# Grouped-query scores as rounded products over all rows, with separate column passes for keys and queries

## Chip, cores and metric

The kernel runs on one core of a Trainium2 chip. The metric is device time in microseconds (us) of one launch. TensorE is written PE, VectorE DVE, ScalarE ACT, GpSimd POOL, and SyncE, which issues DMAs, SP.

## What is computed

The reference is a two-layer diffusion backbone over 512 latent tokens and a context of 256 tokens, D_MODEL = 1024. Each layer mixes tokens by four branches; the one that matters here is grouped-query attention (GQA) with 4 query heads, 2 key heads and a head size of 64:

```python
kc_g, vc_g = rms_norm(split_heads(dc_k, D_KV_HEADS), k_norm), split_heads(dc_v, D_KV_HEADS)
q_g = rope_2d(rms_norm(split_heads(d_q, D_HEADS), q_norm), ang_r, ang_c)
k_g = rope_2d(rms_norm(split_heads(d_k, D_KV_HEADS), k_norm), ang_r, ang_c)
y_d = gqa_latent(q_g, k_g, split_heads(d_v, D_KV_HEADS), kc_g, vc_g)
...
s = jnp.einsum('bqkgd,bskd->bkgqs', qi, k_all).astype(jnp.float32) * d ** -0.5
p = jax.nn.softmax(s, axis=-1).astype(v_all.dtype)
return jnp.einsum('bkgqs,bskd->bqkgd', p, v_all)
```

Latent queries read all 768 keys; in layer 0 context queries read the 256 context keys (no rotary turn for context). The outputs are float32, and so are the scores of the reference.

## The kernel before

Tokens come in TI = 6 tiles of 128: tiles 0 and 1 are context, 2 to 5 latent. `qtiles` is 0 to 5 in layer 0 and 2 to 5 in layer 1, where context has no output. Nearly all matrix products are float32 written as three rounded products (`mm3`, L240 to L247): each operand is split into a rounded high part and a rounded remainder of type float32r, and high by high, high by low and low by high are summed in PSUM. `wload` (L209 to L220) makes the two parts of a weight: ACT casts (L219), DVE subtracts (L220, the weight remainder `wl`).

A static order of instructions per engine is made at build time by the tile framework from its own estimates of durations; each engine then runs its list in order and waits on semaphores. PSUM tiles come from small pools: `pm` 2, `pl` 2, `pq` 3, `po` 1.

`gqa(fill, fill2)` (L1170 to L1254) works in four steps:

1. Keys and values: per tile a projection `tm(W, 0, 256, h, i)` of 24 rounded products of 128x256, whose two halves ACT copies to `k2` and DVE to `v` (both parts of the tile `dkv`).
2. Queries: per tile the same projection, which ACT copies to `q4`.
3. The column pass, per tile: query and key heads together are squared (ACT), summed (DVE), brought through `rsqrt` (L450 to L462: a guess and three Newton rounds of three instructions), scaled by the norm weights, turned by the rotary angles (latent tiles: six DVE operations), transposed on PE (two transposes for queries, two for keys, whose heads ACT has copied twice, L1230) and copied to `qS` (ACT, L1236) and `kS` (DVE, L1237). Here dimensions lie on rows: two heads on two halves of 64 rows. Then `fill()` puts one gate unit into PE's work.
4. Attention, per key head `u` and pair of query tiles (`attend`, L976 to L1033): scores (`qk`, L1242 to L1244), maxima (L987 for context keys, L995 for latent keys), exponentials on ACT (L998, L1001), scaling by the sums, transposes of the probabilities (L1018), copies (L1023), products with the values (L1030). `fill2()` puts one gate unit behind each.

The score products are plain float32 over 64 rows: `mm(out_, qS[rows, u, ...], kS[rows, u, c0:c1])` with `rows` the half of head `hh`. The trace shows each as two passes.

`gate_unit` (L1258) computes sigmoid gates for 128 channels, independent of the attention: 24 products of 128x512 (latent) in both layers, and 24 of 128x256 (context) more in layer 0. There are 32 in a layer; `FILL[4]` and `FILL[5]` are 1.

Of the kernel before, what the change touches and what calls it, by code (L numbers as in the profile page):

```python
# [12 lines left out]
F32R = mybir.dt.float32r  # L13
U8 = mybir.dt.uint8
I32 = mybir.dt.int32
AF = mybir.ActivationFunctionType
ALU = mybir.AluOpType
AX = mybir.AxisListType
# [3 lines left out]
P = 128  # L22
# [5 lines left out]
TI = NT // P  # L28
# [8 lines left out]
EPS = 1e-6  # L37
# [52 lines left out]
def block_kernel(ctx, tc, t, out, dbg=None):  # L90
    nc = tc.nc
# [3 lines left out]
    def mark(label):  # L95
        cur[0] = label
        dbg.get("mark", lambda label: None)(label)
# [14 lines left out]
    def pm():  # L112
        return ps.tile([P, 512], F32, tag="pm", name=nm("pm"), bufs=2)
# [16 lines left out]
    mm = nc.tensor.matmul  # L130
# [217 lines left out]
    def tm(W, col, n, h, i):  # L348

        po = pl()[:, :n]  # L350
        mm3(po, h.sl(i * P, (i + 1) * P), [(a[:, col:col + n], b[:, col:col + n]) for a, b in W])
        return po
# [98 lines left out]
    def rsqrt(z, v, q):  # L451

        V = nc.vector
        V.tensor_scalar(z.bitcast(I32), v.bitcast(I32), -0.5, RS_GUESS, op0=ALU.mult, op1=ALU.add)
        one = z.shape[-1] == 1
        for c in RS:
            if one:
                V.scalar_tensor_tensor(q, z, v, z, op0=ALU.mult, op1=ALU.mult)
            else:
                V.tensor_tensor(q, z, z, op=ALU.mult)  # L460
                V.tensor_tensor(q, q, v, op=ALU.mult)
            V.scalar_tensor_tensor(z, q, -3.0 * c * c, z, op0=ALU.add, op1=ALU.mult)  # L462
# [52 lines left out]
    def mixing(l, h, hpool, W0):  # L515
# [9 lines left out]
        with tc.tile_pool(name=f"mx{l}", bufs=1, reuse_waits="tile") as mp:  # L525
            GB = 1552

            def g6(name, dt=F32):
                return mp.tile([P, GB], dt, tag="g", name=nm(name), bufs=12)


            def s2(shape):

                n = int(np.prod(shape[1:]))
                tl = mp.tile([P, 512], F32, tag="s", name=nm("s"), bufs=11)[:, :n]
                if len(shape) == 2:
                    return tl
                names = ["a", "b", "c", "d"][:len(shape) - 1]
                return tl.rearrange(f"p ({' '.join(names)}) -> p {' '.join(names)}", **dict(zip(names, shape[1:])))

            def small(shape, name, dt=F32, bufs=2):
                return mp.tile(shape, dt, tag=name, name=nm(name), bufs=bufs)
# [627 lines left out]
            def gqa(fill, fill2):  # L1170
                mark("gqa_cols")
                nw = small([P, 2, 64], "dnw", bufs=1)
                nc.scalar.dma_start(nw[:, 0, :], bcast_dram(t["q_norm"][l:l + 1, :], 64))
                nc.scalar.dma_start(nw[:, 1, :], bcast_dram(t["k_norm"][l:l + 1, :], 64))

                qS = g6("dq")[:, :1536].rearrange("p (h s) -> p h s", h=2)
                kS = g6("dk")[:, :1536].rearrange("p (h s) -> p h s", h=2)
                kv = g6("dkv")
                k2 = kv[:, :768].rearrange("p (i h e) -> p i h e", i=TI, h=2)
                v = kv[:, 768:1536].rearrange("p (i c) -> p i c", i=TI)  # L1180
                V = nc.vector
                q4 = g6("dq4")[:, :1536].rearrange("p (i h e) -> p i h e", i=TI, h=4)
                W = wchunk(w_in, [(O_DK, 256)])
                for i in range(TI):
                    po = tm(W, 0, 256, h, i)
                    nc.scalar.copy(k2[:, i], po[:, :128].rearrange("p (h e) -> p h e", h=2))
                    V.tensor_copy(v[:, i, :], po[:, 128:256])
                W = wchunk(w_in, [(O_DQ, 256)])
                for i in qtiles:
                    po = tm(W, 0, 256, h, i)  # L1190
                    nc.scalar.copy(q4[:, i], po.rearrange("p (h e) -> p h e", h=4))
                for i in range(TI):
                    h0 = 0 if i in qtiles else 4
                    x = s2([P, 6, 64])
                    sq = s2([P, 6, 64])
                    if h0 == 0:
                        nc.scalar.activation(sq[:, 0:4], q4[:, i], AF.Square)
                    nc.scalar.activation(sq[:, 4:6], k2[:, i], AF.Square)
                    ms = small([P, 6], "dms", bufs=2)
                    V.tensor_reduce(ms[:, h0:], sq[:, h0:], axis=AX.X, op=ALU.add)  # L1200
                    V.tensor_scalar(ms[:, h0:], ms[:, h0:], 1.0 / 64, EPS, op0=ALU.mult, op1=ALU.add)
                    r = small([P, 6], "drr", bufs=2)
                    c_ = small([P, 6], "drc", bufs=2)
                    rsqrt(r[:, h0:], ms[:, h0:], c_[:, h0:])
                    if h0 == 0:
                        V.tensor_tensor(x[:, 0:4], q4[:, i], r[:, 0:4].unsqueeze(2).to_broadcast([P, 4, 64]), op=ALU.mult)
                    V.tensor_tensor(x[:, 4:6], k2[:, i], r[:, 4:6].unsqueeze(2).to_broadcast([P, 2, 64]), op=ALU.mult)
                    if h0 == 0:
                        V.scalar_tensor_tensor(x[:, 0:4], x[:, 0:4], 0.125, nw[:, 0:1, :].to_broadcast([P, 4, 64]), op0=ALU.mult, op1=ALU.mult)
                    V.tensor_tensor(x[:, 4:6], x[:, 4:6], nw[:, 1:2, :].to_broadcast([P, 2, 64]), op=ALU.mult)  # L1210
                    if i >= 2:
                        yf = s2([P, 384])
                        y = yf.rearrange("p (h r w e) -> p h r w e", h=6, r=2, w=2)
                        x5 = x.rearrange("p h (r w e) -> p h r w e", r=2, w=2)
                        cs = rope[:, i - 2, 0].unsqueeze(1).to_broadcast([P, 6, 2, 16])
                        sn = rope[:, i - 2, 1].unsqueeze(1).to_broadcast([P, 6, 2, 16])
                        t1, t2 = (sq.rearrange("p h (a e) -> p (h a e)", a=2)[:, n * 192:n * 192 + 192].rearrange("p (h r e) -> p h r e", h=6, r=2) for n in range(2))
                        V.tensor_tensor(y[:, :, :, 0], x5[:, :, :, 0], cs, op=ALU.mult)
                        V.tensor_tensor(t1, x5[:, :, :, 1], sn, op=ALU.mult)
                        V.tensor_tensor(y[:, :, :, 0], y[:, :, :, 0], t1, op=ALU.subtract)  # L1220
                        V.tensor_tensor(y[:, :, :, 1], x5[:, :, :, 1], cs, op=ALU.mult)
                        V.tensor_tensor(t2, x5[:, :, :, 0], sn, op=ALU.mult)
                        V.tensor_tensor(y[:, :, :, 1], y[:, :, :, 1], t2, op=ALU.add)
                        yv = yf.rearrange("p (h e) -> p h e", h=6)
                    else:
                        yv = x
                    ts = slice(i * P, (i + 1) * P)
                    po = pm()
                    zk = s2([P, 2, 2, 64])
                    nc.scalar.copy(zk, yv[:, 4:6].unsqueeze(2).to_broadcast([P, 2, 2, 64]))  # L1230
                    for kvh in range(2):
                        if h0 == 0:
                            nc.tensor.transpose(po[:, kvh * P:(kvh + 1) * P], yv[:, 2 * kvh:2 * kvh + 2].rearrange("p h e -> p (h e)"), ident)
                        nc.tensor.transpose(po[:, 256 + kvh * P:384 + kvh * P], zk[:, kvh].rearrange("p w e -> p (w e)"), ident)
                    if h0 == 0:
                        nc.scalar.copy(qS[:, :, ts], po[:, :256].rearrange("p (h s) -> p h s", h=2))  # L1236
                    V.tensor_copy(kS[:, :, ts], po[:, 256:].rearrange("p (h s) -> p h s", h=2))  # L1237
                    fill()
                    mark("gqa_cols")
                new_out(3)  # L1240
                for u in range(2):
                    def qk(out_, hh, i, c0, c1):  # L1242
                        rows = slice(hh * 64, hh * 64 + 64)
                        mm(out_, qS[rows, u, i * P:(i + 1) * P], kS[rows, u, c0:c1], start=True, stop=True)  # L1244

                    def va(hh, kt):
                        return v[:, kt, u * 64:u * 64 + 64]

                    for i2 in aunits:
                        mark("gqa")  # L1250
                        attend(3, u, i2, qk, va)
                        fill2()
# [20 lines left out]
            def fill(k=1):  # L1273
                for _ in range(k):
                    if units:
                        gate_unit(*units.pop(0))
# [113 lines left out]
    h = new_h(hpool)  # L1390
# [376 lines left out]
```

## Time and profile before

| | |
|---|---|
| median of 3 runs | 2494.97 us (2492.56 to 2495.27) |
| profiled execution, its own time | 2492.36 us |
| its span, first to last instruction | 2490.4 us |
| PE busy | 2427.9 us, 97% of the span |
| DVE busy | 1516.3 us, 61% |
| ACT busy | 928.7 us, 37% |
| POOL busy | 149.7 us, 6% |
| chain that ended last | PE 89%, DVE 3%, ACT 2%, DMA 2% |
| layer 0's GQA | some 540 to 760 us |
| layer 1's GQA | some 1840 to 2000 us |

The span lacks 1.96 us of the execution's own time, what lies around the first and last instruction. The chain is followed back from the last instruction to what released each; a high share of one engine says that others were mostly waiting for it. Busy time of a PE instruction reaches past the start of the next one, since products are pipelined: starts in the timeline, not durations, tell its pace.

### The profile page before, as it was taken

To read this page: it belongs to the slowest core of one execution; us is meant where nothing else is said; L and a number is where in the kernel's file an instruction comes from. 1 tells how busy PE (TensorE), PEld (TensorE's weight loads), DVE (VectorE), ACT (ScalarE), POOL (GpSimd) and SP (SyncE) were. 2 spreads that over 40 slices of the span, in tenths; PEclk is the share of its full clock that TensorE was granted. 3 is DMA by queue.
4 is the path that set the end of the run, shared out by engine and by line. 5 is a ranking of instruction groups with operands and counts; after the bars stand their busy time and mean duration, and the time that the engine had idled before them with its cause. 6 is when DMAs were issued, how large, how long until landed. Compare 5 with 4: busy or idle time off the path is not lost.

```text
span 2490.4 us, 41350 instructions
## 1 busy us (share of the span) xinstructions
PE 2427.9 (97%) x16848; PEld 2113.8 (85%) x16848; DVE 1516.3 (61%) x3173; ACT 928.7 (37%) x1638; POOL 149.7 (6%) x225
## 2 busy tenths in 40 slices
PE   7999999999999999999999999999999999999998
PEld 5878888889678989999999988888886688898987
DVE  4477664536447778777764665667566587443436
ACT  3435553333332244334331154456334324322221
POOL 2000000000010040000000030000000102000000
PEclk9999999999999999999999999999999999999999
DMA  7454213213226455232352264322313266333232
GB/s 250 131 162 129 64 36 98 67 58 94 72 85 202 164 164 171 94 113 94 120 183 75 90 194 146 106 70 82 88 57 98 98 195 208 98 94 96 87 95 79
DMA packets 235392, 286.83 MB, mean 115 GB/s; under 512 B 14683, under 2 KB 199107, under 8 KB 235203
## 3 DMA queue, kind: packets, MB, share of 16 engines
q1 hardware_dynamic: 218739, 247.34, 32.3%
q10 hardware_dynamic: 14880, 28.21, 3.1%
q0 software_dynamic: 1584, 8.65, 0.9%
q8 instruction: 132, 2.16, 0.4%
q14 instruction: 57, 0.47, 0.1%
HBM read 246.93 MB, written 35.13 MB: 113 GB/s over the span
## 4 chain that ended last, share of the span: by engine, by line
PE 89%; DVE 3%; ACT 2%; DMA 2%; issue 1%; POOL 1%; SPq 1%; POOLq 0%; ACTq 0%; DVEq 0%
PE pl L245 17%; PE pl L247 17%; PE pl L246 17%; PE pq L245 8%; PE pq L247 8%; PE pq L246 8%; PE po L386 1%; DMA wa<-in_ada_w_dram 1%; PE po L1030 1%; PE pm L1018 1%; PE pq L1244 1%; DMA wf<-in_w_in_dram 1%; PE po L1077 1%; PE pq L1148 1%; PE pm L1065 1%
## 5 line engine op out<-in xcount | busy, mean ns | idle before, releaser
L245 PE MATMUL pl<-h,wh 128*128 128x512 f32 (+2 forms) x1680 | 593.2, 353 | 9.9 <-ACT dtr L597 2.6
L247 PE MATMUL pl<-h,wl 128*128 128x512 f32 (+2 forms) x1680 | 587.1, 350 | 0.0
L246 PE MATMUL pl<-h,wh 128*128 128x512 f32 (+2 forms) x1680 | 586.8, 349 | 0.3 <-DVE h L505 0.3
L220 DVE TENSOR_TENSOR wl<-wf,wh 128x1024 fp32r<-128x1024 f32 x248 | 299.1, 1207 | 316.2 <-ACT wh L219 315.3
L219 ACT CAST wh<-wf 128x1024 fp32r<-128x1024 f32 x248 | 256.2, 1035 | 475.0 <-PE pq L247 195.2
L245 PEld LDWEIGHTS pl<-h,wh 128*128 128x128 f32 x1680 | 320.3, 191 | 61.8 <-issue 11.7
L247 PEld LDWEIGHTS pl<-h,wl 128*128 128x128 f32 x1680 | 320.2, 191 | 44.2 <-issue 9.5
L246 PEld LDWEIGHTS pl<-h,wh 128*128 128x128 f32 x1680 | 320.9, 191 | 37.7 <-issue 5.8
L245 PE MATMUL pl<-wh,h 128*128 128x256 f32 (+1 forms) x1048 | 297.3, 284 | 0.6 <-ACT dtr L597 0.4
L246 PE MATMUL pl<-wl,h 128*128 128x256 f32 (+1 forms) x1048 | 296.2, 283 | 0.0
L247 PE MATMUL pl<-wh,h 128*128 128x256 f32 (+1 forms) x1048 | 296.1, 283 | 0.0
L245 PE MATMUL pq<-h,wh 128*128 128x384 f32 (+2 forms) x640 | 224.8, 352 | 0.0
L247 PE MATMUL pq<-h,wl 128*128 128x384 f32 (+2 forms) x640 | 223.9, 351 | 0.0
L246 PE MATMUL pq<-h,wh 128*128 128x384 f32 (+2 forms) x640 | 223.6, 350 | 0.0
L245 PEld LDWEIGHTS pl<-wh,h 128*128 128x128 f32 x1048 | 198.1, 189 | 4.5 <-issue 1.9
L246 PEld LDWEIGHTS pl<-wl,h 128*128 128x128 f32 x1048 | 198.1, 189 | 3.2 <-issue 2.6
L247 PEld LDWEIGHTS pl<-wh,h 128*128 128x128 f32 x1048 | 198.0, 189 | 2.3 <-issue 2.1
L246 PE MATMUL pq<-wl,h 128*128 128x256 f32 x600 | 169.1, 282 | 0.0
L247 PE MATMUL pq<-wh,h 128*128 128x256 f32 x600 | 169.0, 282 | 0.0
L245 PE MATMUL pq<-wh,h 128*128 128x256 f32 x600 | 168.9, 282 | 0.0
L245 PEld LDWEIGHTS pq<-h,wh 128*128 128x128 f32 x640 | 120.3, 188 | 12.9 <-issue 2.9
L247 PEld LDWEIGHTS pq<-h,wl 128*128 128x128 f32 x640 | 120.2, 188 | 12.6 <-issue 2.0
(469 smaller groups left out, 3820.0 us busy)
## 6 DMA issues: line engine op xcount, KB each, us to landing
wf<-in_w_in_dram SPq DMA_DIRECT2D x120, 512.0 KB, 3.7
wa<-in_ada_w_dram SPq DMA_DIRECT2D x96, 512.0 KB, 4.5
wf<-in_ffn_w_up_dram SPq DMA_DIRECT2D x96, 256.0 KB, 3.5
w<-in_ffn_w_up_dram SPq DMA_DIRECT2D x40, 512.0 KB, 3.7
wf<-in_ffn_w_down_dram SPq DMA_DIRECT2D x36, 512.0 KB, 3.5
gsp<-gs ACTq DMA_DIRECT2D x32, 384.0 KB, 2.5
gld<-gsp SPq DMA_DIRECT2D x16, 768.0 KB, 5.9
ad<-u POOLq DMA_DIRECT2D x11, 768.0 KB, 5.6
```

The lines of the kernel that those rows point to most:

```text
L219: nc.scalar.copy(wh[:, :a * b], wf[:, :a * b])
L220: nc.vector.tensor_tensor(wl[:, :a * b], wf[:, :a * b], wh[:, :a * b].bitcast(F32), op=ALU.subtract)
L245: mm(po, ah, bh, start=(first and k == 0), stop=False)
L246: mm(po, ah, bl, start=False, stop=False)
L247: mm(po, al, bh, start=False, stop=(final and k == n - 1))
L386: mm(po[32 * j:32 * j + 32, :], cT[:, k].rearrange("p r s -> p (r s)"), wf[:, j * 256:(j + 1) * 256], start=(k == 0), stop=(k == KT - 1))
L1018: nc.tensor.transpose(pt[:, (2 * k + j) * P:(2 * k + j + 1) * P], x, ident)
L1030: mm(po[hh * 64:hh * 64 + 64, :], va(hh, k), PT[hh][k], start=(k == 0), stop=(k == nk - 1))
L1065: nc.tensor.transpose(pt[:, (2 * k + j) * P:(2 * k + j + 1) * P], Pj[j][:, (2 * b + k) * P:(2 * b + k + 1) * P], ident)
L1077: mm(po[hh * 64:hh * 64 + 64, cs], va(hh, k) if k < 2 else va(hh, k - 2, i2 + j), PT[hh][k][:, cs], start=(k == 0), stop=(k == 3))
L1148: mm(out_, q3[rows, u, i * P:(i + 1) * P], k3[rows, u, c0:c1], start=True, stop=True)
L1244: mm(out_, qS[rows, u, i * P:(i + 1) * P], kS[rows, u, c0:c1], start=True, stop=True)
```

## The change

The scores become rounded products on all 128 rows. A query tile is split into a rounded high part (ACT copy) and the remainder (DVE subtraction, L1238), set side by side per head, so that after the transpose one head has its high part on rows 0 to 63 and its remainder on rows 64 to 127. Keys are split likewise and each part is doubled on both halves of rows: `kS[0]` is high over high, `kS[1]` low over low. Two accumulating products per score tile then give all four partial products.

The joint column pass is gone. Keys are projected, normed, turned, split, transposed and stored per tile in one loop; then queries in another. Each has its own helper calls: `heads` (ACT copy out of PSUM, square, sum, `rsqrt`, norm weight, rotary turn) and `turned` (four transposes). `fill()` stands in the key loop only. `v` has a tile of its own; `dkv` and `dq4` are gone, and there are two long-lived tiles `dq` and two `dk`. Cut to its core:

```diff
-                qS = g6("dq")[:, :1536].rearrange("p (h s) -> p h s", h=2)
-                kS = g6("dk")[:, :1536].rearrange("p (h s) -> p h s", h=2)
...
+                qS = [g6("dq", F32R)[:, :1536].rearrange("p (h s) -> p h s", h=2) for _ in range(2)]
+                kS = [g6("dk", F32R)[:, :1536].rearrange("p (h s) -> p h s", h=2) for _ in range(2)]
+                v = small([P, TI, P], "dv", bufs=1)
+                def heads(raw, i, n, w, scale):
+                    x = s2([P, n, 64])
+                    sq = s2([P, n, 64])
+                    z = small([P, 3, n], f"dz{n}", bufs=2)
+                    nc.scalar.copy(x, raw.rearrange("p (h e) -> p h e", h=n))
+                    nc.scalar.activation(sq, x, AF.Square)
+                    V.tensor_reduce(z[:, 0], sq, axis=AX.X, op=ALU.add)
+                    V.tensor_scalar(z[:, 0], z[:, 0], 1.0 / 64, EPS, op0=ALU.mult, op1=ALU.add)
+                    rsqrt(z[:, 1], z[:, 0], z[:, 2])
+                    V.tensor_tensor(x, x, z[:, 1].unsqueeze(2).to_broadcast([P, n, 64]), op=ALU.mult)
+                    V.scalar_tensor_tensor(x, x, scale, w.to_broadcast([P, n, 64]), op0=ALU.mult, op1=ALU.mult)
+                    if i < 2:
+                        return x
...
+                def turned(z):
+                    po = pm()
+                    for n in range(4):
+                        nc.tensor.transpose(po[:, n * P:(n + 1) * P], z[:, n * P:(n + 1) * P], ident)
+                    return po.rearrange("p (a h s) -> p a h s", a=2, h=2)
                 W = wchunk(w_in, [(O_DK, 256)])
                 for i in range(TI):
...
                     po = tm(W, 0, 256, h, i)
+                    V.tensor_copy(v[:, i], po[:, 128:256])
+                    y = heads(po[:, :128], i, 2, nw[:, 1:2, :], 1.0)
+                    z = s2([P, 512])
+                    hi, lo = (z[:, a * 256:(a + 1) * 256].rearrange("p (h w e) -> p h w e", h=2, w=2) for a in range(2))
+                    yb = y.unsqueeze(2).to_broadcast([P, 2, 2, 64])
+                    nc.scalar.copy(hi.bitcast(F32R), yb)
+                    V.tensor_tensor(lo, yb, hi, op=ALU.subtract)
+                    po = turned(z)
+                    nc.scalar.copy(kS[0][:, :, ts], po[:, 0])
+                    V.tensor_copy(kS[1][:, :, ts], po[:, 1])
+                    fill()
+                    mark("gqa_cols")
                 W = wchunk(w_in, [(O_DQ, 256)])
                 for i in qtiles:
...
+                    y = heads(tm(W, 0, 256, h, i), i, 4, nw[:, 0:1, :], 0.125)
+                    z = s2([P, 512])
+                    z4 = z.rearrange("p (h w e) -> p h w e", h=4, w=2)
+                    nc.scalar.copy(z4[:, :, 0].bitcast(F32R), y)
+                    V.tensor_tensor(z4[:, :, 1], y, z4[:, :, 0], op=ALU.subtract)
+                    po = turned(z)
+                    nc.scalar.copy(qS[0][:, :, ts], po[:, 0])
+                    V.tensor_copy(qS[1][:, :, ts], po[:, 1])
...
-                        mm(out_, qS[rows, u, i * P:(i + 1) * P], kS[rows, u, c0:c1], start=True, stop=True)
+                        for n in range(2):
+                            mm(out_, qS[u][:, hh, i * P:(i + 1) * P], kS[n][:, u, c0:c1], start=(n == 0), stop=(n == 1))
```

The six rotary operations in `heads` (L1202 to L1207 of the changed kernel) are those of the old pass over 128 elements a row for queries and 64 for keys, where the joint pass had 192.

The scheduler makes a new order in the two GQA stretches and nowhere else. Before, on PE in layer 1, the transposes of one tile (L1233 a query pair, L1234 a doubled key head) stand behind the last product of one gate unit and ahead of the next:

```order
L247 MATMUL pl_2545_18900<-h_1895_14155,wl_2533_18828 128x512
L1233 MATMUL pm_2552_18957<-ident_69,s_2551_18950 128x128
L1234 MATMUL pm_2552_18957<-ident_69,s_2553_18958 128x128
L1233 MATMUL pm_2552_18957<-ident_69,s_2551_18950 128x128
L1234 MATMUL pm_2552_18957<-ident_69,s_2553_18958 128x128
L245 MATMUL pl_2561_18979<-h_1895_14155,wh_2555_18967 128x512
```

The first and the last of these rows belong to gate units of 24 products each (three in a row by high, high and low parts), and so it is between all tiles of the old pass.

Now, on PE in layer 1, behind the transposes of the first query tile q0 (L1213, tile `pm_2586`) and the last four projection products; the rows are scores of the first attention unit (L1246; two rows for each tile are the two accumulating products) and the transposes of q1, q2 and q3 (`pm_2593`, `pm_2600`, `pm_2607`):

```order
L1246 MATMUL pq_2618_19435<-dk_2496_18583,dq_2493_18580 128x512
L1246 MATMUL pl_2619_19436<-dk_2495_18582,dq_2493_18580 128x512
L1246 MATMUL pl_2619_19436<-dk_2496_18583,dq_2493_18580 128x512
L1213 MATMUL pm_2593_19286<-ident_69,s_2592_19283 128x128 x4
L1246 MATMUL pq_2610_19417<-dk_2495_18582,dq_2493_18580 128x256
L1246 MATMUL pq_2610_19417<-dk_2496_18583,dq_2493_18580 128x256
L1246 MATMUL pq_2611_19418<-dk_2495_18582,dq_2493_18580 128x256
L1246 MATMUL pq_2611_19418<-dk_2496_18583,dq_2493_18580 128x256
L1246 MATMUL pl_2623_19454<-dk_2495_18582,dq_2493_18580 128x512
L1246 MATMUL pl_2623_19454<-dk_2496_18583,dq_2493_18580 128x512
L1213 MATMUL pm_2600_19347<-ident_69,s_2599_19344 128x128 x4
L1213 MATMUL pm_2607_19408<-ident_69,s_2606_19405 128x128 x4
```

Five scores stand ahead of the first of these rows: four of 256 columns and one of 512. What moved: no projection and no gate unit stands between q0 and q3 any more; after q3 come two scores and then the next gate unit. In layer 0, where the queries have six tiles q0 to q5, there stand between q1 and q2 four projection products, four scores of 256 columns and 21 projection products; between q2 and q3 three of them, two scores of 256 and 19 gate products of 256; between q3 and q4 five gate products of 256, two scores of 256 and 24 gate products of 512; between q4 and q5 four scores of 512.

On DVE in layer 1, the end of q1's chain and the start of q2's (`dz4` holds the sums and their roots, L1238 is the remainder that q1's transposes wait for):

```order
L995 TENSOR_REDUCE atm_2612_19419<-pq_2618_19435 128x1
L1192 TENSOR_TENSOR s_2588_19257<-s_2588_19257,dz4_2590_19259 128x256
L1193 SCALAR_TENSOR_TENSOR s_2588_19257<-s_2588_19257,dnw_2492_18577 128x256
L1202 TENSOR_TENSOR s_2591_19276<-s_2588_19257,rope_76 128x8x16
L1203 TENSOR_TENSOR s_2589_19258<-s_2588_19257,rope_76 128x128
L1205 TENSOR_TENSOR s_2591_19276<-s_2588_19257,rope_76 128x8x16
L1206 TENSOR_TENSOR s_2589_19258<-s_2588_19257,rope_76 128x128
L1204 TENSOR_TENSOR s_2591_19276<-s_2591_19276,s_2589_19258 128x8x16
L1207 TENSOR_TENSOR s_2591_19276<-s_2591_19276,s_2589_19258 128x8x16
L1238 TENSOR_TENSOR s_2592_19283<-s_2591_19276,s_2592_19283 128x4x64
L1189 TENSOR_REDUCE dz4_2597_19320<-s_2596_19319 128x4
L1190 TENSOR_SCALAR dz4_2597_19320<-dz4_2597_19320 128x4
```

Ahead of these rows, within q1's chain, stand its sum, the guess and nine Newton steps, the copy of q0's turned tile (L1241) and two weight remainders L220. Within q2's chain stand three maxima (L987 twice, L995 once) and four small operations (L996, L997), and within q3's one maximum and two small ones. In layer 0, q2's chain has two maxima L987, q3's two weight remainders, q4's one maximum and q5's two.

## Rows read from the trace of the kernel before

**Rows 1.** The page, busy time of PE (busy us, share of the span, instructions), and shares of its chain by engine:
```profile
PE 2427.9 (97%) x16848; PEld 2113.8 (85%) x16848; DVE 1516.3 (61%) x3173; ACT 928.7 (37%) x1638; POOL 149.7 (6%) x225
...
PE 89%; DVE 3%; ACT 2%; DMA 2%; issue 1%; POOL 1%; SPq 1%; POOLq 0%; ACTq 0%; DVEq 0%
```

**Rows 2.** Windows, old column pass of layer 0 and attention of layer 1:
```profile
core 0: us, PE busy (x) PEld busy (x) DVE busy (x) ACT busy (x) POOL busy (x), PEclk, DMA share, GB/s
568.00:600.00 32.00, 32.00 (x227) 29.80 (x226) 23.23 (x84) 12.13 (x29) 0.00 (x0) 1.00 0.25 77
1919.00:1960.00 41.00, 39.71 (x208) 24.26 (x207) 27.90 (x67) 17.57 (x48) 6.37 (x8) 1.00 0.18 58
```

**Rows 3.** Timeline, PE, layer 0 (start us, us, engine, line, operation, tiles, shapes, count):
```profile
595.05 0.39 PE L247 MATMUL pl<-h,wl 128*128 128x512 f32 x1
595.28 0.39 PE L245 MATMUL pl<-h,wh 128*128 128x512 f32 x1
...
595.97 0.27 PE L1233 MATMUL pm<-ident,s 128*128 128x128 f32 x1
596.08 0.27 PE L1234 MATMUL pm<-ident,s 128*128 128x128 f32 x1
...
596.52 0.28 PE L246 MATMUL pl<-h,wh 128*128 128x256 f32 x1
596.64 0.28 PE L247 MATMUL pl<-h,wl 128*128 128x256 f32 x1
```

**Rows 4.** Groups by form, PE, score products (busy, mean ns | idle before, releaser):
```profile
L1244 PE MATMUL pq<-dk,dq 64*128 64x512 f32 x32 | 18.2, 649 | 8.8 <-ACT s L1001 8.8
```

**Rows 5.** Windows, stretches of lower granted clock in the attention (columns as above):
```profile
652.18:655.59 3.41, 3.41 (x19) 3.41 (x18) 1.94 (x9) 1.90 (x6) 1.08 (x2) 0.50 0.00 0
706.79:710.20 3.41, 3.41 (x18) 3.41 (x18) 1.97 (x8) 2.01 (x8) 1.01 (x2) 0.50 0.00 0
1908.29:1915.12 6.83, 4.76 (x9) 2.67 (x10) 2.17 (x11) 4.35 (x15) 0.00 (x0) 0.50 0.09 31
```

**Rows 6.** Windows of L1244 alone, the GQA stretches of both layers:
```profile
core 0: us, PE busy (x) PEld busy (x), PEclk, DMA share, GB/s
540.00:760.00 220.00, 20.19 (x80) 8.25 (x80) 0.98 0.26 83
1840.00:2000.00 160.00, 18.22 (x64) 7.38 (x64) 0.98 0.28 88
```

**Rows 7.** Timeline, PE, around one group of score products:
```profile
644.81 0.40 PE L247 MATMUL pl<-h,wl 128*128 128x512 f32 x1
645.14 1.56 PE L1244 MATMUL pq<-dk,dq 64*128 64x256 f32 x9
646.11 0.59 PE L1244 MATMUL pl<-dk,dq 64*128 64x512 f32 x1
646.53 0.59 PE L1244 MATMUL pq<-dk,dq 64*128 64x512 f32 x1
646.54 0.59 PE L1244 MATMUL pl<-dk,dq 64*128 64x512 f32 x1
```

**Rows 8.** Timeline, DVE, one tile of the old column pass:
```profile
588.62 0.16 DVE L454 TENSOR_SCALAR drr<-dms 128x6 int32<-128x6 int32 x1
588.82 0.17 DVE L460 TENSOR_TENSOR drc<-drr 128x6 f32<-128x6 f32 x1
...
590.62 0.43 DVE L1206 TENSOR_TENSOR s<-dq,drr 128x256 f32<-128x256 f32 x1
590.96 0.28 DVE L1207 TENSOR_TENSOR s<-dkv,drr 128x128 f32<-128x128 f32 x1
591.16 0.42 DVE L1209 SCALAR_TENSOR_TENSOR s<-s,dnw 128x256 f32<-128x256 f32 x1
```

**Rows 9.** Groups by form, DVE, maxima and weight remainders:
```profile
L220 DVE TENSOR_TENSOR wl<-wf,wh 128x1024 fp32r<-128x1024 f32 x232 | 283.7, 1223 | 280.5 <-ACT wh L219 279.6 <-issue 0.3
...
L987 DVE TENSOR_REDUCE atm<-pq 128x2 f32<-128x512 f32 x24 | 15.6, 684 | 13.5 <-PE pq L1244 13.5
...
L995 DVE TENSOR_REDUCE atm<-pl 128x1 f32<-128x512 f32 x16 | 11.0, 685 | 6.4 <-PE pq L1244 4.0 <-PE pl L1244 2.3
```

**Rows 10.** Groups by form, ACT, the copy that doubles a key tile:
```profile
L1230 ACT COPY s<-s 128x256 f32<-128x256 f32 x12 | 4.9, 405 | 11.3 <-DVE s L1223 9.4 <-DVE s L1210 1.8
```

More of the change, by code (lines that the diff above doesn't have):

```diff
@@ L1174, in gqa @@
                 nc.scalar.dma_start(nw[:, 1, :], bcast_dram(t["k_norm"][l:l + 1, :], 64))
-                qS = g6("dq")[:, :1536].rearrange("p (h s) -> p h s", h=2)
-                kS = g6("dk")[:, :1536].rearrange("p (h s) -> p h s", h=2)
-                kv = g6("dkv")
-                k2 = kv[:, :768].rearrange("p (i h e) -> p i h e", i=TI, h=2)
-                v = kv[:, 768:1536].rearrange("p (i c) -> p i c", i=TI)
-                V = nc.vector
-                q4 = g6("dq4")[:, :1536].rearrange("p (i h e) -> p i h e", i=TI, h=4)
+                qS = [g6("dq", F32R)[:, :1536].rearrange("p (h s) -> p h s", h=2) for _ in range(2)]
@@ new lines, in gqa @@
+                kS = [g6("dk", F32R)[:, :1536].rearrange("p (h s) -> p h s", h=2) for _ in range(2)]
+                v = small([P, TI, P], "dv", bufs=1)
+                V = nc.vector
+                def heads(raw, i, n, w, scale):
[11 more added lines that the diff above has]
+                        return x
+                    yv = s2([P, n, 64])
+                    y = yv.rearrange("p h (r w e) -> p h r w e", r=2, w=2)
+                    x5 = x.rearrange("p h (r w e) -> p h r w e", r=2, w=2)
+                    cs = rope[:, i - 2, 0].unsqueeze(1).to_broadcast([P, n, 2, 16])
+                    sn = rope[:, i - 2, 1].unsqueeze(1).to_broadcast([P, n, 2, 16])
+                    t1, t2 = (sq.rearrange("p h (a e) -> p (h a e)", a=2)[:, m * n * 32:(m + 1) * n * 32].rearrange("p (h r e) -> p h r e", h=n, r=2) for m in range(2))
+                    V.tensor_tensor(y[:, :, :, 0], x5[:, :, :, 0], cs, op=ALU.mult)
+                    V.tensor_tensor(t1, x5[:, :, :, 1], sn, op=ALU.mult)
+                    V.tensor_tensor(y[:, :, :, 0], y[:, :, :, 0], t1, op=ALU.subtract)
+                    V.tensor_tensor(y[:, :, :, 1], x5[:, :, :, 1], cs, op=ALU.mult)
+                    V.tensor_tensor(t2, x5[:, :, :, 0], sn, op=ALU.mult)
+                    V.tensor_tensor(y[:, :, :, 1], y[:, :, :, 1], t2, op=ALU.add)
+                    return yv
@@ L1183, in gqa @@
+                def turned(z):
[3 more added lines that the diff above has]
+                    return po.rearrange("p (a h s) -> p a h s", a=2, h=2)
                 W = wchunk(w_in, [(O_DK, 256)])
                 for i in range(TI):
+                    ts = slice(i * P, (i + 1) * P)
                     po = tm(W, 0, 256, h, i)
-                    nc.scalar.copy(k2[:, i], po[:, :128].rearrange("p (h e) -> p h e", h=2))
@@ L1187, in gqa @@
-                    V.tensor_copy(v[:, i, :], po[:, 128:256])
+                    V.tensor_copy(v[:, i], po[:, 128:256])
[5 more added lines that the diff above has]
+                    V.tensor_tensor(lo, yb, hi, op=ALU.subtract)
@@ L1188, in gqa @@
+                    po = turned(z)
[3 more added lines that the diff above has]
+                    mark("gqa_cols")
                 W = wchunk(w_in, [(O_DQ, 256)])
                 for i in qtiles:
[L1190 to L1226, printed above, removed]
-                    ts = slice(i * P, (i + 1) * P)
[L1228 to L1239, printed above, removed]
@@ L1242, in qk @@
                     def qk(out_, hh, i, c0, c1):
-                        rows = slice(hh * 64, hh * 64 + 64)
-                        mm(out_, qS[rows, u, i * P:(i + 1) * P], kS[rows, u, c0:c1], start=True, stop=True)
+                        for n in range(2):
+                            mm(out_, qS[u][:, hh, i * P:(i + 1) * P], kS[n][:, u, c0:c1], start=(n == 0), stop=(n == 1))
                     def va(hh, kt):
```

## Prediction

> **What bounds the kernel now.** I read the page's top and its chain first. TensorE (PE) is busy for 2427.9 of the span's 2490.4 us, and 89% of the chain that ended last is PE [rows 1]. So whatever PE no longer has to do shortens the run, whatever makes PE wait lengthens it, and work on VectorE (DVE) or ScalarE (ACT) counts only where PE waits for it. The question is then local: does PE wait in the two stretches of grouped-query attention (GQA), one per layer?
>
> The windows answer for the old column passes: from 568 to 600 us PE is busy all 32.00 us while DVE, which does the norm and the rotary turn, has 23.23 us of work [rows 2]. A whole gate unit (`fill`) between two tiles is why: in layer 1 it is 24 products of 512 columns. The timeline gives 0.23 us from one such product's start to the next (595.05 to 595.28), 0.12 for 256 columns (596.52 to 596.64), and 0.11 for a transpose (595.97 to 596.08) [rows 3]. So the unit covers 5.5 us, and in layer 0, with 24 products of 256 columns more, 8.4 us. PE did not wait once there.
>
> In the attention behind, PE did wait: 8.8 us before score products, for exponentials of L1001 [rows 4]. After such waits the granted clock is 0.50 for 3.41, 3.41 and 6.83 us, and PE is busy for 3.41, 3.41 and 4.76 us of these [rows 5]. That is the lower level of 1.2 GHz, and half of 11.58 us, 5.8 us, is lost by it. The old waits cost 14.6 us together.
>
> **The score products.** Alone in the two stretches they keep PE busy for 20.19 + 18.22 = 38.4 us, 144 records: each of 72 fp32 products is two passes on 64 rows [rows 6]. Entering a group costs a little more: the last 512-column product starts at 644.81 and the first score pass at 645.14, 0.33 us where 0.23 is usual [rows 7]. 0.1 us for 24 groups is 2.4 us. After the change there are 144 rounded products on 128 rows, the form that the projections have already: 80 x 0.12 + 64 x 0.23 = 24.3 us. The transposes go from 44 to 88: 44 x 0.11 = 4.8 us more. On PE: 24.3 + 4.8 - 38.4 - 2.4 = **-11.7 us**, or -9.3 if the entry cost stays.
>
> One thing speaks against the move to 128 rows. Passes of two heads on different halves of the rows already start together: 646.53 and 646.54 us [rows 7]. If all 144 ran in such pairs, at 0.43 us a pair of 512 columns (646.11 to 646.54) and half of that, 0.21, a pair of 256, they would take 32 x 0.43 + 40 x 0.21 = 22.2 us, and the change would cost PE 6.9 us in place of saving 11.7. The measured 38.4 us says that many run singly, so I keep -11.7. The Trainium skill, "TensorEngine Tiling (Array Packing)", section "When to Use Tiling", has this as its rule: a contraction of 64 or less calls for 2x row tiling; by that rule alone the sum would have the +6.9.
>
> **The covers that go.** This decides. Projection and column pass are now one, and `fill` stands only in the loop over keys. There it covers: a key tile has its own 24 products (2.9 us) and a gate unit (5.5 or 8.4) against some 4 us on DVE. Between two query tiles only the next projection is left, 2.9 us, and the scheduler has drawn those ahead. In layer 1 PE has 2.3, then 1.4, then 0.44 us of work between the transposes of the four query tiles.
>
> DVE per query tile, from the old tile's timeline [rows 8], start to start: L1190 and the guess L454 0.2 each (588.62 to 588.82); nine Newton steps 1.8 (588.82 to 590.62); two passes over 256 elements 0.34 each (590.62 to 590.96); six rotary passes over 128 elements 0.2 each (590.96 to 591.16). The square sum over 256 elements has no row: it lies below the 0.68 that reductions of 512 take [rows 9] and above 0.2; I take 0.4, nearer the middle. Then DVE needs ACT's rounded copy, 0.41 us for this size [rows 10], with hand-over 0.55, and subtracts, 0.4. That is 5.4 us with rotary and 4.2 without; copying the turned tile out of PSUM is 0.34 more. The copy and the subtraction are new, and not hidden.
>
> Layer 1, from one transpose group to the next, by the order of the rows:
> - q0 to q1: DVE has 5.4 + 0.34, two weight remainders at 1.22 and a maximum of 0.69 [rows 9], 8.9 us; PE has 4 transposes, 4 projection products, 4 scores of 256 and 4 of 512, 2.3. PE waits **6.6**.
> - q1 to q2: 5.4 + 0.34, three maxima (2.05) and four small operations at 0.2, 8.6 us; PE 1.4: **7.2**.
> - q2 to q3: 5.4 + 0.34 + 0.69 + 0.4 = 6.8; PE 0.44: **6.4**.
>
> Together 20.2 us. Layer 0 has six query tiles; two have no rotary turn and two gate halves stand among them. q1 to q2: DVE 7.5, PE 3.9, wait 3.6. q2 to q3, with two weight remainders: 8.6 against 3.3 (19 gate products of 256 in it), wait 5.3. q3 to q4: 6.4 against 6.8 (24 of 512), none. q4 to q5: 7.1 against 1.4, less the 0.4 in hand, wait 5.3. That makes 14.2; DVE may come to q1 about a microsecond early, so 13.
>
> After each run of waits PE should resume at 1.2 GHz. While it waits for DVE anyway that costs nothing; before three gate or projection stretches it costs half of 3.41, 5 us in all [rows 5]. Of the old 14.6 us I let half go, 7: DVE has already taken the first unit's maxima when attention begins, but the later units are as before.
>
> `v` in a tile of its own and the second query and key tiles issue no DMA; they cost nothing, as no instruction in their path is longer. POOL's order is as it was, and SP's but for one weight load that changes places with a gate load; I cost that at nothing, since the waits that end PE's idle time in the old stretches are ACT's, not a DMA's [rows 4].
>
> **Sum:** -11.7 + 20.2 + 13 + 5 - 7 = +19.5 us against the profiled execution's own 2492.36, so **2512 us**. That execution lies 2.6 us below the median 2494.97, inside the spread of the three runs. Less than 0.2%, 5 us, can't be told from no change.
>
> **Rivals.**
> 1. *PE's gain is given back in the attention.* Shorter score groups bring PE sooner to the transposes of the probabilities, which wait for DVE and ACT. For it: DVE is busy for 27.90 of 41.00 us from 1919 to 1960 and ACT for 17.57 [rows 2], in a chain where each unit waits for the one ahead. Against: PE is busy for 39.71 of that window, so something else usually covers. Then neither the 11.7 nor the 7 comes: 20.2 + 13 + 5 = +38, 2530 us; half of it is 2521. Chance 0.2.
> 2. *The other side: DVE keeps up.* DVE comes to the query tiles with a lead of one whole tile, since the keys load it half. For it: 23.23 of 32.00 us busy even in the old pass [rows 2]. A lead of 5.4 us in each layer takes 11 off the waits, and a chain that is 1 us shorter (no hand-over seen, the sum at 0.2) another 6, leaving 16; half clock 2; all of the old 14.6 goes: -11.7 + 16 + 2 - 14.6 = -8, 2484 us. It decides when the new waits come to less than some 19 us. Against: in layer 1 four weight remainders lie in DVE's order ahead of q0 and use the lead up. Chance 0.13.
> 3. *Some of both*: the lead in one layer, two thirds of the old waits gone: about 2493. Chance 0.12.
>
> **How the numbers follow.** The forecast, with +10 to +28 around it, has 0.55. Its low end is the chain at 4.7 us, the old waits all gone; its high end the entry cost kept, none of the old waits gone. To hold 8 in 10 the range leaves out most of rival 2 and the far half of rival 1: 2490 to 2530. Faster by over 0.2% is rival 2, 0.13; within 0.2% is rival 3, 0.12; slower is the rest, 0.75.
>
> **What would show it.** In the profile after: score products' busy time near 24 us; PE waits before L1213 whose releaser is DVE's subtraction L1238, 6 to 7 us each three times in layer 1 and 3 to 5 us in layer 0; none before the transposes of the keys; granted clock of 0.50 near these. Waits at L1213 of less than 19 us would make the forecast wrong, as would waits before the key transposes, or a GQA stretch whose waits for L1001 have grown.

## The result, and the profile after

| | before | after |
|---|---|---|
| median | 2493.76 us (2487.81 to 2495.27, 4 runs) | 2521.43 us (2518.89 to 2523.63, 4 runs) |
| profiled execution, its own time | 2492.36 us | 2523.63 us |
| span | 2490.4 us | 2521.6 us |

The ratio is 1.0121, with a 95% interval of 1.0105 to 1.0137: slower by 1.2%. The forecast was 2512 us, 2490 to 2530, and slower.

The page's first part and the shares of the chain of the changed kernel, to be held against [rows 1]:

```profile
span 2521.6 us, 41680 instructions
PE 2431.3 (96%) x16892; PEld 2129.8 (84%) x16892; DVE 1552.1 (62%) x3373; ACT 937.2 (37%) x1660; POOL 150.9 (6%) x225
...
PE 87%; DVE 4%; ACT 3%; DMA 2%; issue 1%; POOL 1%; SPq 1%; ACTq 0%; POOLq 0%; DVEq 0%
```

PE's busy time has hardly grown, 3.4 us of the 31.2 us that the span is longer. The rest, 27.8 us, is PE standing idle (span less busy time: 62.5 us before, 90.3 after), and the chain goes through DVE and ACT more often. The waits of PE in the changed kernel, from 541 to 790 us (layer 0's GQA) and, behind the dots, from 1840 to 2040 us (layer 1's); the columns are who waited, for whom, us in total, times, longest:

```profile
PE pl L245 <- ACT s L1187: 9.2, 3, 5.1
PE pq L1246 <- ACT s L1001: 1.9, 2, 1.6
PE pm L1213 <- DVE s L1238: 1.8, 1, 1.8
PE pm L1018 <- DVE atm L997: 1.4, 1, 1.4
...
PE pl L1246 <- ACT s L1187: 9.4, 2, 4.7
PE pm L1213 <- DVE s L1238: 5.2, 1, 5.2
PE pl L245 <- ACT s L1187: 2.5, 1, 2.5
PE pm L1018 <- DVE s L1023: 2.0, 3, 1.3
PE pq L1246 <- ACT dq L1240: 0.5, 1, 0.5
```

L1187 and L1188 are ACT's copy of a projection out of PSUM and its square, L1240 ACT's copy of a turned query tile. All that names L1187, L1238 or L1240 lies in the query loops: 9.2 + 1.8 = 11.0 us in layer 0 and 9.4 + 5.2 + 2.5 + 0.5 = 17.6 us in layer 1, **28.6 us**. Before there was nothing of this kind. The waits of the score products for exponentials, 8.8 us before [rows 4], are down to 1.9.

How three query tiles of layer 1 pass, PE from the transposes of q0 and then from the last projection product on:

```profile
1919.81 0.60 PE L1213 MATMUL pm<-ident,s 128*128 128x128 f32 x4
...
1920.60 0.28 PE L247 MATMUL pl<-wh,h 128*128 128x256 f32 x1
1920.87 1.20 PE L1246 MATMUL pq<-dk,dq 128*128 128x256 f32 x6
1926.79 1.22 PE L1246 MATMUL pl<-dk,dq 128*128 128x512 f32 x2 [4.71 <-ACT s L1187]
1927.81 1.05 PE L1213 MATMUL pm<-ident,s 128*128 128x128 f32 x4
1929.33 1.23 PE L1246 MATMUL pq<-dk,dq 128*128 128x256 f32 x4 [0.46 <-ACT dq L1240]
1935.28 1.22 PE L1246 MATMUL pl<-dk,dq 128*128 128x512 f32 x2 [4.73 <-ACT s L1187]
1936.30 1.06 PE L1213 MATMUL pm<-ident,s 128*128 128x128 f32 x4
1942.57 1.09 PE L1213 MATMUL pm<-ident,s 128*128 128x128 f32 x4 [5.21 <-DVE s L1238]
1943.31 1.20 PE L1246 MATMUL pq<-dk,dq 128*128 128x512 f32 x2
```

From one group of transposes to the next, counting from q0's at 1919.81: 8.0, 8.5 and 6.3 us. PE does little in these times and waits in all three. The two longest waits ahead of q1 and q2 end with ACT's L1187, not with DVE's L1238. ACT's own rows say why, at 1926 us:

```profile
1926.06 0.40 ACT L1237 CAST s<-s 128x256 fp32r<-128x256 f32 x1 [4.09 <-DVE s L1207]
1926.37 0.36 ACT L1187 COPY s<-pl 128x256 f32<-128x256 f32 x1
1926.77 0.42 ACT L1188 ACTIVATE s<-s 128x256 f32<-128x256 f32 x1
```

ACT stands still for 4.09 us for DVE's last rotary operation, since the rounded copy L1237 is next in its order; the copy that empties the next projection's PSUM tile stands behind. So PE waits for a buffer, the buffer for ACT, and ACT for DVE. DVE at the same place:

```profile
1925.74 0.28 DVE L1207 TENSOR_TENSOR s<-s,s 128x128 f32<-128x128 f32 x1
1926.50 0.43 DVE L1238 TENSOR_TENSOR s<-s,s 128x256 f32<-128x256 f32 x1 [0.47 <-ACT s L1237]
1927.22 0.42 DVE L1189 TENSOR_REDUCE dz<-s 128x4 f32<-128x256 f32 x1 [0.29 <-ACT s L1188]
```

Between two tiles DVE itself waits twice, 0.47 us for the rounded copy and 0.29 us for the next tile's square, which stands behind that copy on ACT.

The clock follows, in windows (busy times, then the granted clock, DMA share, GB/s):

```profile
632.84:639.52 6.68, 6.23 (x29) 6.12 (x29) 3.98 (x18) 2.23 (x5) 0.00 (x0) 0.50 0.00 0
642.92:649.76 6.84, 4.71 (x22) 4.71 (x23) 5.56 (x26) 1.09 (x3) 0.00 (x0) 0.50 0.27 77
1916.10:1919.52 3.42, 3.42 (x18) 3.42 (x18) 1.74 (x9) 1.06 (x2) 0.00 (x0) 0.50 0.00 0
1926.34:1946.82 20.48, 9.63 (x28) 7.01 (x29) 14.44 (x59) 6.99 (x23) 0.00 (x0) 0.50 0.01 2
```

PE works for 6.23 + 4.71 + 3.42 + 9.63 = 24.0 us at half the clock, which loses 12.0 us in the two GQA stretches, where 5.8 were lost before [rows 5]. Each of these windows lies in or behind the new waits.

### The profile page after: what moved, and what is told of

Its sections match the earlier page's. It is cut to its first block, busy times and chain, and to the rows that moved or that the text cites. A ratio compares the mean times of both kernels' runs of the same rounds, so it can differ in the third digit from the quotient of the medians.

```text
span 2521.6 us, 41680 instructions
## 1 busy us (share of the span) xinstructions
PE 2431.3 (96%) x16892; PEld 2129.8 (84%) x16892; DVE 1552.1 (62%) x3373; ACT 937.2 (37%) x1660; POOL 150.9 (6%) x225
## 4 chain that ended last, share of the span: by engine, by line
PE 87%; DVE 4%; ACT 3%; DMA 2%; issue 1%; POOL 1%; SPq 1%; ACTq 0%; POOLq 0%; DVEq 0%
PE pl L245 16%; PE pl L247 16%; PE pl L246 16%; PE pq L245 8%; PE pq L247 8%; PE pq L246 8%; PE po L386 1%; DMA wa<-in_ada_w_dram 1%; PE po L1030 1%; DMA wf<-in_w_in_dram 1%; PE po L1077 1%; PE pq L1148 1%; PE pm L1018 1%; PE pm L1065 1%; ACT wh L219 1%
## 5 line engine op out<-in xcount | busy, mean ns | idle before, releaser
L220 DVE TENSOR_TENSOR wl<-wf,wh 128x1024 fp32r<-128x1024 f32 x248 | 299.1, 1207 | 314.1 <-ACT wh L219 313.0
L245 PEld LDWEIGHTS pl<-wh,h 128*128 128x128 f32 x1048 | 200.0, 191 | 12.4 <-ACT s L1187 7.2
```

The lines of the kernel that those rows point to most:

```text
L220: nc.vector.tensor_tensor(wl[:, :a * b], wf[:, :a * b], wh[:, :a * b].bitcast(F32), op=ALU.subtract)
L245: mm(po, ah, bh, start=(first and k == 0), stop=False)
```

## Experiments

The cover theory is the prediction's: the query loop has no independent work for PE between two tiles, so DVE's chain shows. Rivals: the PSUM buffers that the waits name; and the split into two parts itself, wherever the gate units stand. Every kernel was timed against the kernel before on the same chip. That kernel's median was 2490.07 us in the first four experiments, 2490.06 in the next three and 2491.34 in the last. The changed kernel was not timed again beside them; a difference from its 2521.43 us sets two sets of runs against each other.

**A gate unit behind the query tiles too.**

```diff
                     V.tensor_copy(qS[1][:, :, ts], po[:, 1])
+                    fill()
+                    mark("gqa_cols")
```

> One edit to the changed kernel: fill() behind each query tile too, so a gate unit stands between query tiles again (the units are taken from those that stood behind the later attention units). Cover theory (PE waits in the query loop because no independent PE work stands between two query tiles while DVE works off one): the 28.6 us of waits between query tiles and most of the 12 us that the lower clock costs go; the last attention units have no gate unit left and give 5 to 15 us back: 2490 to 2502 us. PSUM theory (PE waits for pl buffers because the copy L1187 stands behind the rounded copy on ACT): gate units use pl too, so the waits stay, over 2512 us.

Measured: 2493.59 us, ratio 1.0009 (0.9998 to 1.0020). One helper call takes back the loss, to within the spread. The waits of PE from 1835 to 2030 us:

```profile
PE pm L1213 <- DVE s L1238: 5.1, 1, 5.1
PE pm L1018 <- DVE s L1023: 2.8, 5, 1.1
PE pl L1248 <- ACT gs L1270: 1.4, 1, 1.4
```

One wait of 5.1 us is left, before the last query tile, where the scheduler's order has only half a gate unit (12 products) and eight score products between the transposes of the last two query tiles; in layer 0 none that names the query tiles' chain. PSUM buffers are used as before, and the waits for L1187 are gone, so the number of buffers alone does not make PE wait.

**The gate units moved from the keys to the queries.**

```diff
                     V.tensor_copy(kS[1][:, :, ts], po[:, 1])
-                    fill()
-                    mark("gqa_cols")
...
                     V.tensor_copy(qS[1][:, :, ts], po[:, 1])
+                    fill()
+                    mark("gqa_cols")
```

> The changed kernel with fill() moved from the key loop to the query loop, 10 gate units in the column passes in place of 12. Cover theory: the query waits (28.6 us and the lower clock) go, but a key tile now has 2.9 us of projection on PE against some 4.2 us and a share of weight remainders on DVE, so 1 to 2 us of waiting for each of 12 key tiles: 2500 to 2510 us. PSUM theory: the query waits stay, 2515 us or more.

Measured: 2505.93 us, ratio 1.0065 (1.0045 to 1.0086). Most of the waits change sides: five, 11.7 us in all, now stand before the transposes of the keys (L1224 is ACT's rounded copy of keys); L1236, the queries' subtraction, is left with one of 9.0 us. Layer 0 stands ahead of the dots, layer 1 behind:

```profile
PE pm L1213 <- ACT s L1224: 6.5, 3, 3.4
...
PE pm L1213 <- DVE s L1236: 9.0, 1, 9.0
PE pm L1213 <- ACT s L1224: 5.2, 2, 4.5
```

The 9.0 us stand where the scheduler's order has nothing at all between the transposes of the last two query tiles, although the source has a `fill()` there:

```profile
1905.98 0.60 PE L1213 MATMUL pm<-ident,s 128*128 128x128 f32 x4
1915.59 1.11 PE L1213 MATMUL pm<-ident,s 128*128 128x128 f32 x4 [9.01 <-DVE s L1236]
```

**Separate passes with the old scores.** Splitting, doubling into two parts and rounded products are undone; the two loops stay.

```diff
-                    z = s2([P, 512])
-                    z4 = z.rearrange("p (h w e) -> p h w e", h=4, w=2)
-                    nc.scalar.copy(z4[:, :, 0].bitcast(F32R), y)
-                    V.tensor_tensor(z4[:, :, 1], y, z4[:, :, 0], op=ALU.subtract)
-                    po = turned(z)
-                    nc.scalar.copy(qS[0][:, :, ts], po[:, 0])
-                    V.tensor_copy(qS[1][:, :, ts], po[:, 1])
+                    nc.scalar.copy(qS[:, :, ts], turned(y.rearrange("p h e -> p (h e)")))
```

> The changed kernel with the scores put back: float32 products on 64 rows, no high and low parts, two transposes a tile; separate passes for keys and queries stay. Cover theory: the query chain on DVE is shorter by the subtraction (0.42), the hand-over to ACT's rounded copy (0.55) and the copy L1241 (0.34), 1.3 us for each of some seven waits, so 9 us of waits go; PE work is about the same: 2508 to 2516 us, still well above before. Rival (the split into two parts costs the time, not the separate passes): 2492 to 2500 us.

Measured: 2505.26 us, ratio 1.0055 (1.0036 to 1.0073), a little below the range given. The separate passes alone cost 0.55%; the split makes the same passes dearer by another 16 us (2521.43 - 2505.26). The waits agree: those of its query loops come to 2.6 + 0.8 us in layer 0 and 4.4 + 3.0 + 1.6 in layer 1, 12.4 us where the changed kernel has 28.6. That is more than the 9 us expected. A likely part of it is ACT's order: with the split, the rounded copy stands ahead of the next tile's copy and square, and DVE waits for both (0.47 and 0.29 us in the rows above); that this explains the rest is not shown.

**Two Newton rounds fewer for queries.**

```diff
-                    rsqrt(z[:, 1], z[:, 0], z[:, 2])
+                    rsqrt(z[:, 1], z[:, 0], z[:, 2], RS[:1] if n == 4 else RS)
```

> The changed kernel with one Newton round of three for the queries' root (two rounds are left out, so the roots are less exact): six DVE instructions of 0.2 us, 1.2 us, less per query tile. Cover theory: DVE's chain sets PE's waits, 1.2 us less for each of six or seven: 7 to 9 us less, 2512 to 2515 us. If something else sets them (ACT's order, PSUM buffers): no change, 2519 to 2523 us.

Measured: 2513.00 us, ratio 1.0083 (1.0066 to 1.0101): 8.4 us less than the changed kernel. Ten query tiles save 1.2 us of DVE each, 12 us, and two thirds of it comes out at the end. The waits for L1187 and L1238, layer 0 ahead of the dots and layer 1 behind:

```profile
PE pl L245 <- ACT s L1187: 3.3, 2, 2.0
PE pm L1213 <- DVE s L1238: 3.1, 1, 3.1
...
PE pl L1246 <- ACT s L1187: 6.9, 2, 3.5
PE pm L1213 <- DVE s L1238: 4.0, 1, 4.0
PE pl L245 <- ACT s L1187: 1.2, 1, 1.2
```

They come to 18.5 us, where the changed kernel has 28.1. Those that name ACT's L1187 shrink with DVE's chain too. DVE, 62% busy over the span, sets the time here.

**Query projections in the larger pool.**

```diff
-                    y = heads(tm(W, 0, 256, h, i), i, 4, nw[:, 0:1, :], 0.125)
+                    y = heads(tm(W, 0, 256, h, i, pq), i, 4, nw[:, 0:1, :], 0.125)
```

> The changed kernel with the query projections in the pool pq (3 buffers) in place of pl (2). Cover theory: PE runs one projection further and then waits for DVE all the same, at the transposes (L1213) in place of the projections; the sum of the waits and the time stay: 2517 to 2524 us. PSUM theory: the 21 us of waits for L1187 go and nothing takes their place: 2498 to 2503 us.

Measured: 2517.24 us, ratio 1.0109 (1.0093 to 1.0125). Layer 0 and, behind the dots, layer 1:

```profile
PE pq L1246 <- ACT s L1187: 6.7, 2, 3.9
PE pm L1213 <- DVE s L1238: 6.2, 1, 6.2
...
PE pq L1246 <- ACT s L1187: 9.5, 2, 4.8
PE pm L1213 <- DVE s L1238: 6.5, 2, 5.2
```

The sum is 28.9 us, where L1187 and L1238 had 28.1 in the changed kernel. The larger pool moves part of the waiting from L1187 to L1238 and removes none; the time lies within the spread of the changed kernel's. The PSUM theory's 2498 to 2503 us did not come. The run alone does not settle it, since `pq` also takes scores, and 16.2 us of waits still name L1187; with the gate units put back and the shorter DVE chain, which take such waits away or shorten them without a buffer more, the theory falls.

**Rounded scores in the joint pass.** The kernel before, with only the scores, the split and the transposes changed; one pass over keys and queries with a gate unit behind each tile.

```diff
+                    z = s2([P, 512])
+                    hi, lo = (z[:, a * 256:(a + 1) * 256].rearrange("p (h w e) -> p h w e", h=2, w=2) for a in range(2))
+                    yb = yv[:, 4:6].unsqueeze(2).to_broadcast([P, 2, 2, 64])
+                    nc.scalar.copy(hi.bitcast(F32R), yb)
...
-                        rows = slice(hh * 64, hh * 64 + 64)
-                        mm(out_, qS[rows, u, i * P:(i + 1) * P], kS[rows, u, c0:c1], start=True, stop=True)
+                        for n in range(2):
+                            mm(out_, qS[u][:, hh, i * P:(i + 1) * P], kS[n][:, u, c0:c1], start=(n == 0), stop=(n == 1))
```

> The kernel before with only the scores changed: rounded products on 128 rows, high and low parts, doubled keys, 88 transposes; projections first and then one joint column pass with a gate unit behind each tile, as before. Cover theory: the gate units cover DVE in layer 0 (8.4 us each against some 7.7 us of DVE) and nearly in layer 1 (6.4 us against 7.7 and a share of weight remainders), so at most some 2.5 us of waiting for each of four tiles there, against some 5 us less work on PE: 2486 to 2498 us. Rival (the split itself costs the time, wherever the cover stands): 2508 us or more.

Measured: 2489.62 us, ratio 1.0001 (0.9991 to 1.0010). The split costs nothing that shows where the cover stands. But no gain shows in the time either. The rounded products' own windows, as in [rows 6] for the products before:

```profile
540.00:760.00 220.00, 17.25 (x80) 12.18 (x80) 0.98 0.27 87
1840.00:2000.00 160.00, 14.15 (x64) 9.72 (x64) 0.99 0.29 92
```

31.4 us busy in place of 38.4. Busy time is not what they cost, though: it counts the end of a group's last product while the next product already runs. Six products here are busy for 0.87 us, and the next one starts after 0.71:

```profile
655.06 0.87 PE L1256 MATMUL pq<-dk,dq 128*128 128x256 f32 x6
655.77 0.39 PE L245 MATMUL pl<-h,wh 128*128 128x512 f32 x1
```

The waits over the whole span for exponentials (8.8 before [rows 4]) and the probabilities' transposes:

```profile
PE pq L1256 <- ACT s L1001: 9.1, 3, 4.3
...
PE pm L1018 <- DVE s L1023: 4.1, 6, 1.4
```

The old waits are still there, and 4.1 us before the probabilities' transposes are new. On the page PE is busy for 2418.3 of 2488.2 us. That is 9.6 us less busy time than before (3.7 of them since the lower clock cost less in this execution: half of PE's busy time at a granted clock of 0.50 is 15.0 us, and was 18.7), but 7.4 us more idle time, 4.1 of these in the two GQA stretches. So there is a gain on PE, and waiting takes most of it back; the span is 2.2 us shorter, and the timed runs show no difference.

**Half of the key tiles with a gate unit.**

```diff
-                    fill()
+                    if i % 2:
+                        fill()
                     mark("gqa_cols")
```

together with the unit behind each query tile. 

> fill() behind every query tile and behind every second key tile, which leaves more gate units to the attention than a unit behind every tile does (2493.6 us). Cover theory: two key tiles have some 11 us on DVE against 12 to 15 us on PE with one gate unit, so keys stay covered, and the last attention units have a gate unit again: 2485 to 2491 us, at or a little below the kernel before. If the cover of the attention is worth nothing: 2492 to 2496 us, as with a unit behind every tile.

Measured: 2492.63 us, ratio 1.0013 (1.0003 to 1.0023). No gain over a unit behind every tile: layer 1 still waits 6.6 us for one L1239 (the queries' subtraction) and 2.3 us before a key tile's transposes. The 6.6 us stand before the last query tile, and the order has nothing between its transposes and those of the tile ahead (1907.89 and 1915.14 us). The expectation of 2485 to 2491 was missed; the time lies in the range of the other one, that the cover of the attention is worth nothing.

**The joint pass, two units behind each attention unit of layer 1.**

```diff
-FILL1 = (12, 2, 1, 0, 1, 1)
+FILL1 = (12, 2, 1, 0, 1, 2)
```

> The joint pass with rounded scores (2489.6 us, the same as before) with two gate units in place of one behind each attention unit of layer 1, taken from the four units that stand at the end of the stretch. If the work that rounded scores save on PE is given back in the attention for want of cover (7 us of waits for L1001 and L1023 in layer 1), some 3 us of it come back: 2484 to 2488 us. If the units do as much good at the end, where they cover the last unit's chain: 2488 to 2491 us, no change.

Measured: 2488.00 us, ratio 0.9991 (0.9981 to 1.0001). The interval touches 1, so whether this version beats the kernel before stays open; its waits in layer 1 (4.3 us for L1001, 4.6 for L1023) are no smaller in the profiled execution, so the cover of the attention is not shown to be the reason. That execution was the slowest of the twelve, 2493.47 us.

## Why the prediction was right, and where its terms were off

- **Direction and cause: right.** The forecast's deciding step was that `fill` stands only in the key loop. With the units put back between query tiles the time is that of the kernel before, within the spread; with the units moved most of the waits move; with DVE's chain shortened the time falls. The number is closer than its terms: the query waits were 4.6 us too high and the other terms together 16.3 too low, and that these cancel in part is luck.
- **Query waits: 20.2 + 13 us forecast, 17.6 + 11.0 measured.** Of the measured ones 2.5 us ahead of q0 in layer 1 and 1.4 ahead of q1 in layer 0 were not forecast; the forecast ones came to 15.1 and 9.6. The periods between transposes in layer 1 were forecast as 8.9, 8.6 and 6.8 us and are 8.0, 8.5 and 6.3. Waits came out shorter than these say, since PE did its work between them at half the clock. What the forecast had wrong is the releaser of most: it expected L1238, and the trace names L1187. The prediction saw DVE's chain and not that ACT's order ties the next projection's PSUM buffer to it. By the letter of its own sign, less than 19 us at L1213, it would have been wrong: only 1.8 + 5.2 = 7.0 us stand there, and the rest stands before the products that want the buffer.
- **No waits before the key transposes: right** in the changed kernel; without their gate units they appear.
- **The clock: +5 us forecast for new stretches, and half of the old 5.8 gone with the old waits; measured in the two GQA stretches 12.0 us lost in place of 5.8, so +6.2.** The mechanism held, the size did not.
- **Old waits in the attention: 8.8 us for L1001 went to 1.9**, but 3.4 us before the probabilities' transposes (1.4 for L997, 2.0 for L1023) came instead.
- **PE's own work: -11.7 us forecast; this is the term that was most off.** The forecast set a busy time of the old products, 38.4 us, against a pace from start to start of the new ones, 24.3. In like terms the joint pass shows 38.4 and 31.4 us of busy time; or 36.9 and 28.1 us, if the times from each score product's start to the next product's start are added up, less PE's idle time between them. The cost of entering a group did go: in the joint pass the product ahead of a group starts 0.23 us before it (661.98 to 662.21), where it was 0.33. With that and the transposes as the forecast counted them, 28.1 - 36.9 - 2.4 + 4.8 = -6.4 us. The balance over the whole span agrees. PE's busy time on the page, less half of what it did at a granted clock of 0.50, is 2427.9 - 18.7 = 2409.2 us before, 2418.3 - 15.0 = 2403.3 in the joint pass (5.9 less) and 2431.3 - 23.6 = 2407.7 in the changed kernel (1.5 less). Why the new products take 28.1 us and not 24.3, and why even less is left in the changed kernel, was not tried by itself. The sign "score products' busy time near 24 us" failed: it is 33.8 us in the changed kernel.
- The rule set against the change (the Trainium skill, "TensorEngine Tiling (Array Packing)", section "When to Use Tiling": 2x row tiling for a contraction of 64) did not decide it. The old passes on two halves took 36.9 us from start to start, not the 22.2 of full pairs, so they were only partly side by side in this kernel, and the products over all rows took 28.1.
- Of the 31.2 us by which the span grew, 19.5 were forecast. The span's growth is 27.8 us of idle time and 4.9 of the lower clock (18.7 to 23.6 over the whole span), less 1.5 of work. Of the 11.7 us that are missing, the gain on PE that did not come is 10.2 and the clock 2.8; the query waits, shorter by 4.6 than forecast, take that much back; the last 3.3 are idle time besides the query waits, which fell by 0.8 us where about 4 was forecast. Rival 1 (the gain on PE does not arrive) described the size, +38 us in full, half of it +29. Its mechanism, waits in the attention, is borne out in part, with 4.1 us at L1018 in the joint pass and 3.4 in the changed kernel, but most of the changed kernel's loss stands in the query loops. Rival 2 (DVE keeps up) is refuted: the new waits are 28.6 us, not under 19.

## What to carry to other kernels

Filler work on the busiest engine belongs between the steps of every loop that has a long chain on another engine; when a loop is split in two, the filler has to be split with it, and its count is a budget (here 32 units a layer). The call in the source is not enough: where the scheduler's order left nothing between two query tiles, 9.0 and 6.6 us of waiting stayed. An engine with 62% of busy time can set the end wherever the cover is missing, and a wait that names a buffer can be that same chain, seen through the order of a third engine. A saving on the bound engine has to be counted in one measure: busy time of the old products against the start-to-start pace of the new ones made a gain of 11.7 us where some 6 were there.

## What was not expected of the hardware

While PE waited in pieces, with small groups between, the clock stayed low for long: from 1926.34 to 1946.82 us it was granted 0.50 throughout, 20.48 us in which PE was busy for 9.63. So the small groups ran at 1.2 GHz: four transposes took 0.74 us from their start to the next product's (1942.57 to 1943.31) where four had taken 0.35 at full clock (1919.81 to 1920.16). Part of a wait is thus taken up by slower work and does not show as idle time: the waits measured fell short of the periods, though the periods came out nearly as forecast.
